# A recurrence's heads with other mixers' work between their steps: 2.0 units for each of their own instead of 1.15

## The chip, the cores and the metric

The kernel runs on one core of a Trainium2 chip. The metric is the device time of one launch in microseconds (us); the inputs lie in the chip's memory and the result is written there. The core has a matrix engine (TensorE, PE in the profile; PEld is its weight loading), a vector engine (VectorE, DVE), a scalar engine (ScalarE, ACT), a general one (GpSimd, POOL) and queues of DMA, most of which SyncE (SP) issues. Each engine works through its own list of instructions in order and waits at semaphores for the others.

## The reference

A sequence of 512 tokens of width 1024 goes through two layers of a first block (gated feed-forward, three mixers side by side, gated feed-forward) and two layers of a second block (three other mixers, then an MLP). Only the mixers of the first block matter here:

```python
def mixers(h):                              # one layer, S = 512, d = 1024
    z_a, z_b, z_c = split_cols(h @ w_in, [...])
    o_a = rwkv7_mixer(z_a, ...)             # 4 heads of 64, a recurrence in both directions
    o_b = mla_mixer(z_b, ...)               # latent attention, 8 heads
    o_c = retention_mixer(z_c, ...)         # 4 heads, in chunks
    return concatenate([o_a, o_b, o_c], -1) @ w_out

# rwkv7_mixer
    def step(state, inp):
        w_t, kk_t, kka_t, k_t, v_t, r_t = inp
        sk = einsum('dbhvk,dbhk->dbhv', state, kk_t)
        new = (state * w_t[..., None, :] - sk[..., :, None] * kka_t[..., None, :]
               + v_t[..., :, None] * k_t[..., None, :])
        ...
    y = head_norm(y, RWKV_LN_EPS) * ln_g + ln_b
    return (y + bonus).reshape(B, S, RWKV_WIDTH) * g
```

The recurrence (`rwkv7_mixer`) is computed for two directions and four heads, then normed by head, scaled, shifted, given a bonus term and gated. All of it is in f32.

## The kernel before

Activations lie transposed, 128 channels by 512 tokens. A large product is made of three fp32r matmuls: each operand is split into a rounded half (ACT) and its remainder (DVE, `split`, L446; `mix_r...` tiles in the profile). Weights come by DMA into `raw` and are split into pairs of `wr` tiles in the same way (`weight`, L385), some three ahead of their use. Small products are plain f32 matmuls, which the trace records twice. Nearly every instruction is issued through one helper (L138), so the trace's rows are told apart by tile names.

`mixer1` (L1441) computes the three mixers of a layer with Python generators that issue instructions and yield a number, the work that they have issued. `merge` (L1427) takes a main generator and a filling one. For every number that the main one yields it runs the filling one until that has yielded as much; what is left of the filling when the main one ends is issued at the end, and what is left of the main one when the filling ends follows without filling.

The main one is `rwkv` (L1111). After preparations it makes two generators `rwkv_heads` (L1042), one for each pair of heads (j = 0 and 1), and advances them by turns. Each does eight steps of the chunked recurrence; before every second step stands an `rwkv_pair` (L952), which prepares two steps. After the eighth come a square (ACT), a sum and an inverse root (`rsqrt`, L455, eleven small operations of DVE), a product, a broadcast (`head_bcast`, L744: one copy on DVE, four PE transposes), the bonus product, a gate matmul; then four transposes of y, a scaling from PSUM, an addition and the gate product (L1104 to L1108). Each generator yields 40 in all, 80 for both, and `rwkv` multiplies what they yield by `HEADS_FILL` (L1135).

The filling one (`fill`, L1453) issues the projections of the three mixers, then `retention` (L1377), then `mla` (L1249, latent attention). `mla` goes through eight heads, each with a first part (maxima of the scores, `mla_first`, L1177) and a second (`mla_second`, L1204: four blocks of three score matmuls, an exponential on ACT and four value matmuls of 65 columns), and transposes each pair of heads (`mla_pair`, L1235). At its last head it splits what the other two mixers have put out by then (`split_all`, L1304).

After `merge`, whatever isn't yet split is split (L1468), and `out_proj` (L418) multiplies by the output weights, eight blocks of 128 rows. The operands of each block are taken in the order `oa + oc + ob` (L1474): the recurrence's two outputs first, then the retention's two, then latent attention's four.

A scheduler orders each engine's instructions once more, within what the program's order and the buffers allow, so that independent matmuls of a later block can stand ahead of ones that have to wait.

Of the kernel before, what the change touches and what calls it, by code (L numbers as in the profile page):

```python
# [29 lines left out]
D_FF2 = 4096  # L30
NF2 = D_FF2 // P
FF_GROUPS = ((0, 8), (8, 7), (15, 7))
HEADS_FILL = 1.15
INV_WAIT = 20
HEAD_STEP = 1.5
INV_STEP = 2.5
# [199 lines left out]
class Build:  # L236
# [874 lines left out]
    def rwkv(self, l, z, dv, out):  # L1111
# [17 lines left out]
        while runs:  # L1129
            for g in list(runs):  # L1130
# [3 lines left out]
                else:  # L1134
                    yield need * HEADS_FILL  # L1135

# [864 lines left out]
```

## Time and profile before

| | us |
|---|---|
| median of three runs | 3496.72 (3494.79 to 3498.40) |
| profiled execution | 3498.36 |
| its span in the trace | 3496.6 |
| PE busy in it | 3398.2 |
| DVE busy | 2086.3 |
| ACT busy | 1427.3 |

The span is what the trace's clock covers from the first to the last instruction; all times in the rows count from its start. Busy time is the sum of an engine's instructions without overlap. Matmuls are pipelined and their ends are modelled, so a PE that is busy throughout can still hold pauses of some tenths of a us; they show in the distance from one start to the next. The granted clock of PE has two levels, 1.0 (2.4 GHz) and 0.5 (1.2 GHz); a stretch's figure is a mean of them. The mixers of the first block stand at about 410 to 810 us (layer 0) and 1560 to 1960 us (layer 1), their last third as described above at 583 to 800 and 1725 to 1945.

### The profile page before, as it was taken

To read this page: it belongs to the slowest core of one execution; us is meant where nothing else is said; L and a number is where in the kernel's file an instruction comes from. 1 tells how busy PE (TensorE), PEld (TensorE's weight loads), DVE (VectorE), ACT (ScalarE), POOL (GpSimd) and SP (SyncE) were. 2 spreads that over 40 slices of the span, in tenths; PEclk is the share of its full clock that TensorE was granted. 3 is DMA by queue.
4 is the path that set the end of the run, shared out by engine and by line. 5 is a ranking of instruction groups with operands and counts; after the bars stand their busy time and mean duration, and the time that the engine had idled before them with its cause. 6 is when DMAs were issued, how large, how long until landed. Compare 5 with 4: busy or idle time off the path is not lost. (4 is left out here: it accounts for less than half of the span.)

```text
span 3496.6 us, 45680 instructions
## 1 busy us (share of the span) xinstructions
PE 3398.2 (97%) x17394; PEld 2785.5 (80%) x17394; DVE 2086.3 (60%) x4249; ACT 1427.3 (41%) x2626; POOL 158.0 (5%) x272
## 2 busy tenths in 40 slices
PE   6999999999999999999999999999999999999998
PEld 5888877788888888887678888887788887778887
DVE  7954694767964544468476544467754446774445
ACT  3233554454233423245355423345443344443333
POOL 2000101001000000010100000000000000100000
PEclk9999998999999999999799999999999999999999
DMA  7933332016842222233201222221122222112222
GB/s 272 334 139 105 125 91 58 25 55 225 318 174 98 89 97 92 100 121 95 64 20 47 87 97 94 98 95 62 61 91 97 97 97 74 68 67 100 98 97 73
DMA packets 132876, 375.73 MB, mean 107 GB/s; under 512 B 37712, under 2 KB 41072, under 8 KB 132656
## 3 DMA queue, kind: packets, MB, share of 16 engines
q1 hardware_dynamic: 127808, 359.48, 29.8%
q0 software_dynamic: 3776, 12.32, 1.0%
q8 instruction: 136, 2.23, 0.3%
q10 hardware_dynamic: 1072, 1.01, 0.1%
q14 instruction: 84, 0.69, 0.1%
HBM read 362.27 MB, written 10.49 MB: 107 GB/s over the span
## 5 line engine op out<-in xcount | busy, mean ns | idle before, releaser
L138 ACT CAST wr<-raw 128x512 fp32r<-128x512 f32 (+2 forms) x1054 | 642.6, 611 | 1527.3 <-PE ps L138 1400.6
L138 DVE TENSOR_TENSOR wr<-raw,wr 128x512 fp32r<-128x512 f32 (+2 forms) x1048 | 707.5, 678 | 737.2 <-ACT wr L138 708.4
L138 PE MATMUL ps<-ff_h,wr 128*128 128x512 f32 (+1 forms) x4296 | 959.1, 385 | 12.5 <-ACT ff_h L138 8.2
L138 PEld LDWEIGHTS ps<-ff_h,wr 128*128 128x128 f32 x4296 | 792.8, 190 | 175.2 <-ACT ff_h L138 11.0
L138 PE MATMUL ps<-mlp_r,wr 128*128 128x512 f32 (+1 forms) x3120 | 699.4, 386 | 2.1 <-ACT mlp_r L138 2.1
L138 PEld LDWEIGHTS ps<-mlp_r,wr 128*128 128x128 f32 x3120 | 578.6, 188 | 121.2 <-ACT mlp_r L138 3.0
L138 PE MATMUL ps<-ff_r,wr 128*128 128x512 f32 (+1 forms) x2238 | 483.0, 377 | 0.0
L138 PEld LDWEIGHTS ps<-ff_r,wr 128*128 128x128 f32 x2238 | 403.6, 188 | 77.6
L138 PE MATMUL ps<-mix_r,wr 128*128 128x512 f32 (+1 forms) x1104 | 275.4, 400 | 3.3 <-DVE mix_s L138 1.7
L138 PE MATMUL ps<-mix_h_x,wr 128*128 128x512 f32 (+2 forms) x1104 | 260.6, 395 | 5.0 <-ACT mix_h_x L138 2.2
L138 PEld LDWEIGHTS ps<-mix_r,wr 128*128 128x128 f32 (+1 forms) x1104 | 200.6, 186 | 55.3 <-issue 3.5
L138 PEld LDWEIGHTS ps<-mix_h_x,wr 128*128 128x128 f32 (+1 forms) x1104 | 198.6, 196 | 52.8 <-issue 7.8
L138 DVE SCALAR_TENSOR_TENSOR ff_big<-ff_big,ff_big 128x1024 f32<-128x1024 f32 x144 | 175.9, 1234 | 12.6 <-DMA ff_big<-in_w_ada 12.4
L138 DVE SCALAR_TENSOR_TENSOR ff_s<-ff_s,ps 128x512 f32<-128x512 f32 x176 | 119.9, 682 | 82.7 <-PE ps L138 78.6
L138 DVE SCALAR_TENSOR_TENSOR x<-ps,hg,x 128x512 f32<-128x512 f32 (+1 forms) x102 | 73.2, 718 | 78.6 <-PE ps L138 78.5
L138 DVE TENSOR_TENSOR ps<-ps,mlp_s 128x512 f32<-128x512 f32 (+1 forms) x66 | 45.1, 683 | 100.3 <-PE ps L138 100.3
L138 DVE TENSOR_TENSOR mlp_r<-mlp_s,mlp_r 128x512 fp32r<-128x512 f32 x80 | 54.6, 691 | 68.2 <-ACT mlp_r L138 68.2
L138 PE MATMUL ps<-mix_s,mix_s 128*128 128x128 f32 (+6 forms) x632 | 87.5, 291 | 3.2 <-ACT mix_s L138 3.1
L138 ACT ACTIVATE mix_s<-ps,m 128x128 f32<-128x128 f32 (+3 forms) x130 | 65.4, 517 | 52.1 <-PE ps L138 28.1
L138 DVE TENSOR_REDUCE m<-ps 128x1 f32<-128x512 f32 (+4 forms) x132 | 74.8, 585 | 18.7 <-PE ps L138 18.2
L138 ACT COPY mix_s<-ps 64x128 f32<-64x128 f32 (+7 forms) x138 | 54.5, 399 | 74.8 <-PE ps L138 50.2
L138 PEld LDWEIGHTS ps<-mix_s,mix_s 128*128 128x128 f32 (+5 forms) x632 | 64.7, 175 | 21.5 <-ACT mix_s L138 12.6
(313 smaller groups left out, 3234.6 us busy)
## 6 DMA issues: line engine op xcount, KB each, us to landing
raw<-in_ff_in SPq DMA_DIRECT2D x176, 512.0 KB, 3.4
ff_big<-in_w_ada SPq DMA_DIRECT2D x144, 512.0 KB, 6.2
raw<-in_mlp SPq DMA_DIRECT2D x128, 512.0 KB, 3.4
raw<-in_ff_out SPq DMA_DIRECT2D x64, 448.0 KB, 3.2
raw<-in_ff_out SPq DMA_DIRECT2D x32, 512.0 KB, 3.8
raw<-in_out SPq DMA_DIRECT2D x32, 512.0 KB, 3.4
raw<-in_in SPq DMA_DIRECT2D x28, 512.0 KB, 3.4
raw<-in_in_a SPq DMA_DIRECT2D x18, 512.0 KB, 4.0
```

The lines of the kernel that those rows point to most:

```text
L138: self.alloc.last[self.name] = f(*a, **k)
```

## The change

```diff
-HEADS_FILL = 1.15
+HEADS_FILL = 2.0
```

Nothing else differs. Over the heads `rwkv` now yields 160 units for 80 of its own instead of 92. It concerns both layers of the first block, in the same way; the rest of the program stays as it is, but for buffer numbers. The order of the instructions follows from it, and these are three places of layer 0. In the names, `ps` are PSUM tiles, `mix_1_s` f32 tiles of the mixers, `mix_1_r`, `_r_x` and `_r_y` halves of split operands, `mix_1_va` the attention's values, `m` small columns; the last two numbers of a row are the shape that is written.

PE at the end of latent attention, before. The value matmuls of the last head, blocks 2 and 3, with the start of the projection around them; the four transposes by `ident` are the last `mla_pair`:

```order
L138 MATMUL ps_114<-mix_1_va_w_2_4744,mix_1_s_2669 128x65 x4
L138 MATMUL ps_113<-mix_1_r_x_3_4763,wr_74 128x512
L138 MATMUL ps_114<-mix_1_va_w_3_4745,mix_1_s_2677 128x65 x4
L138 MATMUL ps_113<-mix_1_r_x_2_4762,wr_74 128x512
L138 MATMUL ps_113<-mix_1_r_x_3_4763,wr_73 128x512
L138 MATMUL ps_113<-mix_1_r_y_1_4752,wr_74 128x512
L138 MATMUL ps_113<-mix_1_r_y_0_4751,wr_74 128x512
L138 MATMUL ps_117<-ident,mix_1_s_w_1_4747 128x128 x4
L138 MATMUL ps_113<-mix_1_r_y_1_4752,wr_73 128x512
L138 MATMUL ps_113<-mix_1_r_y_3_4754,wr_74 128x512
```

PE at the same place now. The two matmuls into `ps_116` are the last step of the second pair of heads; `mix_1_s_2678` and `mix_1_s_2683` are the broadcasts of the bonus, `mix_1_s_2674` the gates, `mix_1_s_2667` the last `mla_pair`, and `mix_1_s_2682` and `mix_1_s_2685` are y of the two pairs; `mix_1_r_y_5` and `_4` are the halves of the recurrence's first output:

```order
L138 MATMUL ps_116<-mix_1_s_2676,mix_1_s_2681 128x128 x2
L138 MATMUL ps_118<-mix_1_va_w_3_4591,mix_1_s_2668 128x65 x4
L138 MATMUL ps_112<-ident,mix_1_s_2678 128x128 x4
L138 MATMUL ps_119<-mix_1_s_2673,mix_1_s_2674 128x512
L138 MATMUL ps_117<-ident,mix_1_s_2667 128x128 x4
L138 MATMUL ps_113<-ident,mix_1_s_2683 128x128 x4
L138 MATMUL ps_115<-mix_1_s_2673,mix_1_s_2674 128x512
L138 MATMUL ps_114<-ident,mix_1_s_2682 128x128 x4
L138 MATMUL ps_118<-mix_1_r_y_5_4602,wr_74 128x512
L138 MATMUL ps_118<-mix_1_r_y_4_4601,wr_74 128x512
L138 MATMUL ps_118<-mix_1_r_y_5_4602,wr_73 128x512
L138 MATMUL ps_116<-ident,mix_1_s_2685 128x128 x4
```

The transposes of y stood 125 to 140 rows ahead of the projection's first matmul; now they stand directly before it and behind its first three. Six matmuls later comes the first one that takes the recurrence's second output.

DVE, before, at the end of the recurrence: `mix_1_s_2685` is y of the second pair, `mix_1_s_w_0` and `mix_1_s_2674` the two outputs, the rest is latent attention's and one weight:

```order
L138 TENSOR_REDUCE m_87<-ps_114 128x1
L138 TENSOR_TENSOR mix_1_s_2685<-mix_1_s_2685,m_94 128x512
L138 TENSOR_SCALAR mix_1_s_w_0_4746<-ps_112,vec 128x512
L138 TENSOR_SCALAR mr_104<-m_87 128x4
L138 TENSOR_TENSOR mix_1_s_w_0_4746<-mix_1_s_w_0_4746,mix_1_s_2677 128x512
L138 TENSOR_TENSOR wr_71<-raw_65,wr_72 128x512
L138 TENSOR_TENSOR mix_1_s_w_0_4746<-mix_1_s_w_0_4746,mix_1_s_2670 128x512
L138 TENSOR_SCALAR mix_1_s_2674<-ps_119,vec 128x512
L138 TENSOR_TENSOR mix_1_r_x_11_4771<-ps_118,mix_1_r_x_10_4770 64x512
L138 TENSOR_TENSOR mix_1_s_2674<-mix_1_s_2674,mix_1_s_2666 128x512
L138 TENSOR_TENSOR mix_1_r_x_13_4773<-ps_117,mix_1_r_x_12_4772 64x512
L138 TENSOR_TENSOR mix_1_s_2674<-mix_1_s_2674,mix_1_s_2682 128x512
```

DVE now: the end of the second pair's inverse root, the splits of the two outputs (`mix_1_r_y_4`, `mix_1_r_x_7`) and the first weight of the projection:

```order
L138 SCALAR_TENSOR_TENSOR m_87<-m_87,m_86 128x8
L138 SCALAR_TENSOR_TENSOR m_94<-m_87,m_94 128x8
L138 TENSOR_TENSOR m_87<-m_94 128x8
L138 TENSOR_TENSOR mix_1_r_y_4_4601<-mix_1_s_2666,mix_1_r_y_5_4602 128x512
L138 SCALAR_TENSOR_TENSOR m_87<-m_87,m_86 128x8
L138 SCALAR_TENSOR_TENSOR m_94<-m_87,m_94 128x8
L138 TENSOR_TENSOR mix_1_s_2685<-mix_1_s_2685,m_94 128x512
L138 TENSOR_SCALAR mix_1_s_2669<-ps_116,vec 128x512
L138 TENSOR_TENSOR mix_1_s_2669<-mix_1_s_2669,mix_1_s_w_1_4593 128x512
L138 TENSOR_TENSOR mix_1_s_2669<-mix_1_s_2669,mix_1_s_w_0_4592 128x512
L138 TENSOR_TENSOR mix_1_r_x_7_4613<-mix_1_s_2669,mix_1_r_x_6_4612 128x512
L138 TENSOR_TENSOR wr_73<-raw_64,wr_74 128x512
```

Latent attention's operations, which stood between those of the recurrence, are gone from the place, and the splits, which came some twenty rows later, follow at once.

PE at the end of the retention, before. `ident` with `mix_1_s_x` are the broadcasts of the retention's norm, `x_131` with `mix_1_s_2670` and `mix_1_s_2687` belong to a pair of the recurrence, and `mix_1_r_y` with `wr` is latent attention's first product:

```order
L138 MATMUL ps_115<-mix_1_s_2680,mix_1_s_x_0_4169 64x64 x8
L138 MATMUL ps_118<-x_131,mix_1_s_2670 128x128
L138 MATMUL ps_112<-ident,mix_1_s_x_2_4171 128x128 x4
L138 MATMUL ps_119<-ident,mix_1_s_x_3_4172 128x128 x4
L138 MATMUL ps_118<-x_131,mix_1_s_2670 128x128 x3
L138 MATMUL ps_114<-mix_1_s_2687,mix_1_s_2684 128x128
L138 MATMUL ps_117<-mix_1_r_y_0_4751,wr_74 128x512
```

Now:

```order
L138 MATMUL ps_115<-mix_1_s_2680,mix_1_s_y_3_2723 64x64 x8
L138 MATMUL ps_118<-x_134,mix_1_s_2668 128x128 x4
L138 MATMUL ps_115<-x_130,mix_1_s_2675 128x128 x4
L138 MATMUL ps_113<-ident,mix_1_s_x_0_4169 128x128 x4
L138 MATMUL ps_114<-ident,mix_1_s_x_2_4171 128x128 x4
L138 MATMUL ps_117<-mix_1_r_y_0_4597,wr_74 128x512
```

The pair's matmuls that stood between the broadcasts and the first product now stand ahead of the broadcasts.

## Rows read from the trace of the kernel before

**Rows 1.** The page, busy time of each engine, share of the span, instructions.
```profile
PE 3398.2 (97%) x17394; PEld 2785.5 (80%) x17394; DVE 2086.3 (60%) x4249; ACT 1427.3 (41%) x2626; POOL 158.0 (5%) x272
```

**Rows 2.** The page, chain that ended last, shares of the span by engine.
```profile
PE 42%; DVE 2%; ACT 1%; issue 0%; POOL 0%; DVEq 0%; ACTq 0%; POOLq 0%
```

**Rows 3.** Stretches: length; busy PE, PEld, DVE, ACT, POOL; granted PE clock; DMA.
```profile
583.00:647.00 64.00, 61.32 (x535) 45.31 (x533) 49.81 (x139) 28.02 (x71) 6.76 (x24) 1.00 0.01 2
647.00:693.00 46.00, 45.27 (x356) 37.64 (x356) 37.76 (x91) 28.25 (x62) 3.61 (x7) 1.00 0.14 47
693.00:713.00 20.00, 20.00 (x143) 17.81 (x144) 15.89 (x57) 9.21 (x16) 0.55 (x1) 1.00 0.05 14
713.00:763.00 50.00, 49.26 (x315) 41.92 (x313) 31.30 (x59) 29.99 (x52) 3.83 (x7) 1.00 0.19 59
...
1725.00:1790.00 65.00, 62.63 (x502) 43.39 (x500) 44.91 (x120) 26.21 (x65) 7.23 (x24) 0.95 0.02 6
```

**Rows 4.** PE's waits from 583 to 647 us: total, times, longest.
```profile
PE ps L138 <- ACT mix_s_y L138: 1.1, 1, 1.1
```

**Rows 5.** PE in order of time: start, length, operation, count; in the retention.
```profile
630.66 1.07 PE L138 MATMUL ps<-mix_s_x,mix_s 128*64 128x512 f32 x2
631.66 0.66 PE L138 MATMUL ps<-mix_s_x,mix_s_x 64*64 64x128 f32 x8
```

**Rows 6.** PE in order of time, around the end of the recurrence's last step.
```profile
703.53 0.66 PE L138 MATMUL ps<-mix_s,mix_s 128*128 128x128 f32 x4
...
704.67 0.61 PE L138 MATMUL ps<-mix_va_w,mix_s 128*128 128x65 f32 x4
705.11 0.61 PE L138 MATMUL ps<-ident,mix_s 128*128 128x128 f32 x4
705.56 1.02 PE L138 MATMUL ps<-mix_s,x 128*128 128x512 f32 x2
706.02 1.96 PE L138 MATMUL ps<-mix_r_x,mix_r_x 97*128 97x512 f32 x6
```

**Rows 7.** DVE in order of time, norm and gate of the recurrence's heads.
```profile
704.24 0.59 DVE L138 TENSOR_TENSOR mix_s<-mix_s,ps 64x128 f32<-64x128 f32 x2
...
707.31 0.42 DVE L138 TENSOR_TENSOR mix_s_w<-ps,m 128x256 f32<-128x256 f32 x1
...
708.53 0.48 DVE L138 SCALAR_TENSOR_TENSOR m<-m,m 128x8 f32<-128x8 f32 x4
...
709.04 0.69 DVE L138 TENSOR_TENSOR mix_s<-mix_s,m 128x512 f32<-128x512 f32 x1
709.65 0.68 DVE L138 TENSOR_TENSOR mix_r_x<-ps,mix_r_x 128x512 fp32r<-128x512 f32 x1
...
714.77 0.80 DVE L138 TENSOR_SCALAR mix_s_w<-ps,vec 128x512 f32<-128x512 f32 x1
...
720.49 0.67 DVE L138 TENSOR_TENSOR mix_s<-mix_s,mix_s 128x512 f32<-128x512 f32 x1
...
736.35 0.69 DVE L138 TENSOR_TENSOR mix_r_x<-mix_s_w,mix_r_x 128x512 fp32r<-128x512 f32 x1 [2.52 <-PE ps L138]
```

**Rows 8.** ACT in order of time, rounding of the recurrence's output.
```profile
735.70 0.62 ACT L138 CAST mix_r_x<-mix_s_w 128x512 fp32r<-128x512 f32 x1 [1.45 <-PE ps L138]
```

**Rows 9.** DVE in order of time, the retention's norm.
```profile
641.80 0.39 DVE L138 SCALAR_TENSOR_TENSOR m<-m,m 128x16 f32<-128x16 f32 x2
```

**Rows 10.** PE in order of time, start of the output projection.
```profile
762.93 0.48 PE L138 MATMUL ps<-mix_r_x,wr 128*128 128x512 f32 x1
...
767.12 3.57 PE L138 MATMUL ps<-mix_r_x,wr 128*128 128x512 f32 x15
```

**Rows 11.** Stretches as in rows 3, where the granted clock falls.
```profile
397.00:400.50 3.50, 0.98 (x7) 0.64 (x6) 2.84 (x13) 1.16 (x3) 1.19 (x3) 1.00 0.96 369
400.50:407.50 7.00, 6.51 (x29) 6.21 (x30) 6.04 (x20) 5.59 (x12) 2.74 (x4) 0.52 0.26 97
...
544.00:575.00 31.00, 29.37 (x256) 22.94 (x257) 4.37 (x8) 10.02 (x24) 2.77 (x8) 0.50 0.24 47
```

## The prediction

> **What bounds the kernel now.** I read the page first: TensorE (PE) is busy in 97% of the span [rows 1], and the chain that ended last lies on PE and hardly anywhere else [rows 2]. So a change of order can give only what PE idles, and takes whatever it makes PE wait. Then the stretches of one mixer, layer 0 [rows 3]: 583 to 647 us is the retention mixed with two thirds of the recurrence's pairs; 647 to 693 and 693 to 713 latent attention with the rest of the recurrence; 713 to 763 latent attention by itself; from 763 the output projection. PE idles 2.7 + 0.7 + 0.0 + 0.7 = 4.1 us in the four; the last row of the group, the retention's stretch in layer 1, is like layer 0's. The largest wait in the first stretch is 1.1 us [rows 4]. VectorE (DVE) has 49.8 of 64 us to do there and 31.3 of 50 in the stretch without recurrence. That difference is all that a better mixture can live on.
>
> Some idling is hidden in modelled ends: the retention's one f32 matmul (two records) at 630.66 has its successor at 631.66, 1.00 us later [rows 5], while a gate matmul of as many columns is followed after 0.46 [rows 6]. If all 16 such matmuls of a layer (2 pairs of heads, 4 blocks, 2 heads) hid the same 0.54, that is 8.6 us more. So a layer has between 4 and 13 us to be gained.
>
> **What is moved.** No instruction is added or removed in number; the main generator asks for 160 units of other work over its heads instead of 92. The retention stretch keeps two pairs and four steps of each head pair, and latent attention starts after them. But the filling work now ends before the main work: as the order shows, the last steps of the recurrence come immediately before latent attention's last value matmuls, and behind these there is nothing but the output projection, whose first operands are the recurrence's own outputs. Queues of DMA are passed by nothing: the weights' loads stand in the same order on SP.
>
> **Before, the recurrence's tail cost nothing.** Its last state add is at 704.24, its last gate product at 720.49 and the split of its outputs at 735.70 and 736.35, while the first projection matmul runs at 762.93 [rows 7, 8, 10]. The 17 us of norm, transposes and gate lay beside latent attention, and some 26 us were to spare.
>
> **The tail now, from the end of the second head pair's last step (T).** DVE's queue, as the order prints it, holds from there to the split of the last output: twelve passes over 128x512 at 0.61 (709.04 to 709.65), 7.3; two scalings from PSUM at 0.80, 1.6; the state add 0.59; a 128x256 product 0.42; ten small operations at 0.12 that are interleaved (four took 0.48), 1.2; and seven of a single chain at 0.2 (two took 0.39 in the retention's norm, where nothing stands between them), 1.4 [rows 7, 9]. Sum 12.5. It waits for two things: PE's transposes of the second pair, 0.45 and handovers, 0.6; and ScalarE's rounding of its output ahead of the last split, 0.62 and a handover, 0.7 [rows 8]. So T + 13.8 for the last split; the projection's three matmuls that need only the rounded half cover the last 0.6, and PE is wanted again from T + 13.2.
>
> PE's own work up to there: four value matmuls, eight records, 0.88 (four in 0.44); five times four transposes at 0.45, 2.25; two gate matmuls at 0.46, 0.92 [rows 6]; nine projection matmuls at 0.24 (fifteen took 3.57) [rows 10], 2.2. Sum 6.2. PE idles 13.2 - 6.2 = 7.0 us per layer, in four pieces: about 4 before the first output is rounded, 0.7 for its low half, 0.6 for the second product, 1.6 before the second output is rounded. Bounds: 6, if handovers vanish and everything overlaps; 9, if the ten interleaved operations cost 0.2 too and ScalarE's queue is late once.
>
> **The clock.** At 397 to 400.5 PE is busy for 0.98 of 3.5 us, and in the next 7 us the granted clock is 0.52, so nearly all of them run at the lower of its two levels, 1.2 instead of 2.4 GHz [rows 11]. The new tail has about 2 us of work in the 7 from T + 3 on, so I expect one such stretch behind it in each layer. It overlaps partly with the later pauses; with 3 us of work in it, doubled work costs 1.5. Ends: 0, and 3.5 for a full stretch of 7 us.
>
> **The seam.** Latent attention's first gemm now stands directly behind the retention's norm transposes; before, four 128x128 matmuls of a pair stood between, eight records of about 0.11 (four records of one step took 0.66, the last one's modelled end included) [rows 6], 0.9 us. That cover is gone: 0.9, ends 0 and 1.5.
>
> **The gain in the middle.** The stretch without recurrence gets steps to mix in, but it idles only 0.7. The retention stretch, where the idling is, loses filling: its DVE work stays while the pairs beside it go, so its mixture becomes denser on DVE, not thinner. I take 1.5 us gained per layer, near the recorded idling and not the hidden; ends 4 gained (all that is recorded) and 3 lost.
>
> Sum per layer: 7.0 + 1.5 + 0.9 - 1.5 = 7.9; two layers, 15.8. The profiled run took 3498.4 (span 3496.6), which is 1.6 above the median, so 3514 for it and **3513** against the median. Low end: 6 + 0 + 0 - 4 = 2 per layer, 3501; high end: 9 + 3.5 + 1.5 + 3 = 17, 3531.
>
> A rule that speaks for the change: the Trainium skill, "Perfetto Trace Analysis", section "Optimization Strategy", says that a kernel whose most contended engine changes over time may gain from interleaving its regimes. The trace has such regimes, 49.8 of 64 us on DVE against 31.3 of 50 [rows 3], but the one that is heavy on DVE is not the one that gets new partners. By the rule alone the sum would be rival A's.
>
> **Rivals.**
> A. The mixture wins. If all of the 13 us vanish, the rest (7.0 + 1.5 + 0.9 = 9.4) is paid back and 3.6 us per layer are left: 3490; with the tail at its floor and no slow clock, 3485. For: DVE's unequal load. Against: the gain would have to come from the stretch that loses partners. It decides from a gain of 9.4 per layer, twice my upper end. Chance 0.05.
> B. A wash. The tail at its floor of 6, no slow clock, a gain of 3 to 4: 3500 to 3503. Chance 0.14.
> C. The slow clock stays. From 544 to 575 PE had half the clock over 31 us, although it was busy for 29.4 of them [rows 11]. If the projection ran so for as long, 15 us more per layer: about 3540. Against: there the matmuls were small; behind the tail come dense ones of 512 columns. The Trainium skill, "TensorE: Matmul & The Clock Gate", section "What's actually happening", says that the throttled state is the default and that activity releases it, which by itself would favour a short stretch; the trace agrees for dense work, 7 us with PE busy in 6.5 of them from 400.5 on [rows 11]. Chance 0.06.
> D. The change doesn't do what it says, in time: the tail is covered by something the order doesn't show, say matmuls that PE still has in its queue. 3497. Against: behind the last value matmul nothing independent is left. Chance 0.03.
>
> **How the numbers follow.** The forecast (tail uncovered, 2 to 17 us per layer and over 0.2% in all) has 0.72. About 0.2%, 7 us, is what a measurement of this kernel can tell from no change: that is 3490 to 3504. Faster: A, 0.05. Within: B and D, 0.17. Slower: forecast and C, 0.78. The range, 3500 to 3530, takes in the bounds of the terms and most of B; A, C and D are left out.
>
> **What would show it.** Right: in both layers, between the last value matmuls and the projection, PE waits of about 4 and 1.6 us for ScalarE's mix_r and of 0.6 each for DVE; DVE without a gap through that time; granted clock of 0.5 behind it; the whole mixer longer by 8 us. Wrong: a tail without pauses over 1 us (then D or B); PE idling under 1 us and no 1.00 us spacing in the retention (then A); a projection at half clock for over 10 us (then C). The prediction falls if the four pieces add up to under 4 us, or if the retention's stretch changes by more than 4.

## The result and the profile after

The changed kernel takes 3534.2 us (median of four, 3528.4 to 3537.9) against 3497.6 (3494.8 to 3502.7): a ratio of 1.0107, with an interval of 1.0093 to 1.0122. It is slower, as forecast, but by 37 us instead of 16, and outside the range (3500 to 3530). The profiled execution is the fastest of the four: 3528.4, its span 3526.6. In it, the time from the start of the retention's stretch to the first product of the next block (583.3 to 812.0 in layer 0 before, 584.6 to 830.2 now) is 245.6 us in layer 0 and 247.1 in layer 1, against 228.7 in both before. These 16.9 and 18.4 us are nearly the whole loss; the two profiled executions differ by only 30.0 in all, as the changed one is 5 us shorter elsewhere.

The end of a mixer in layer 0, PE in order of time (start, length, operation, count, idle time before and what ended it), the counterpart of [rows 6, 10]:

```profile
770.38 1.00 PE L138 MATMUL ps<-mix_va_w,mix_s 128*128 128x65 f32 x8
...
774.26 0.66 PE L138 MATMUL ps<-ident,mix_s 128*128 128x128 f32 x4
778.42 0.50 PE L138 MATMUL ps<-mix_r_y,wr 128*128 128x512 f32 x1 [3.51 <-ACT mix_r_y L138]
779.26 1.22 PE L138 MATMUL ps<-mix_r_y,wr 128*128 128x512 f32 x2 [0.33 <-DVE mix_r_y L138]
780.27 1.10 PE L138 MATMUL ps<-ident,mix_s 128*128 128x128 f32 x4
781.03 2.20 PE L138 MATMUL ps<-mix_r_y,wr 128*128 128x512 f32 x6
784.44 2.15 PE L138 MATMUL ps<-mix_r_x,wr 128*128 128x512 f32 x8 [1.21 <-ACT mix_r_x L138]
```

The recurrence's last step ends at 770.4, then come the last value matmuls, broadcasts and gates, and the projection starts at 778.42 after a pause of 3.51 for ScalarE's rounding of the first output. Its second operand follows at 784.44 after 1.21. Layer 1 shows the same two, 3.53 and 1.04. From the last step to 784.44 are 14.1 us, with 5.05 of recorded pauses; before, PE had no pause there. DVE works through most of the time, with two pauses at the end, 1.21 for PE and 0.74 for ScalarE:

```profile
778.52 0.68 DVE L138 TENSOR_TENSOR mix_r_y<-mix_s,mix_r_y 128x512 fp32r<-128x512 f32 x1
...
779.51 0.69 DVE L138 TENSOR_TENSOR mix_s<-mix_s,m 128x512 f32<-128x512 f32 x1
781.41 0.81 DVE L138 TENSOR_SCALAR mix_s<-ps,vec 128x512 f32<-128x512 f32 x1 [1.21 <-PE ps L138]
782.26 1.42 DVE L138 TENSOR_TENSOR mix_s<-mix_s,mix_s_w 128x512 f32<-128x512 f32 x2
784.42 0.69 DVE L138 TENSOR_TENSOR mix_r_x<-mix_s,mix_r_x 128x512 fp32r<-128x512 f32 x1 [0.74 <-ACT mix_r_x L138]
```

These are the first output's split, the second pair's product, scaling, additions and split, the sequence that the order showed.

That is only a part of the loss. The retention's stretch in pieces (columns as in rows 3), which answers to the first of [rows 3]:

```profile
589.00:600.00 11.00, 10.64 (x56) 5.18 (x56) 9.45 (x16) 3.13 (x8) 1.36 (x4) 1.00 0.00 0
600.00:604.80 4.80, 4.44 (x60) 3.86 (x58) 4.04 (x12) 3.02 (x7) 1.77 (x5) 1.00 0.01 3
604.80:615.00 10.20, 10.20 (x43) 9.52 (x44) 5.91 (x25) 2.89 (x6) 0.00 (x0) 0.50 0.00 0
615.00:618.40 3.40, 1.24 (x8) 0.62 (x6) 2.85 (x7) 0.95 (x1) 0.00 (x0) 1.00 0.00 0
618.40:622.00 3.60, 3.60 (x7) 1.27 (x7) 2.82 (x11) 0.52 (x2) 0.00 (x0) 0.53 0.00 0
622.00:641.00 19.00, 18.83 (x153) 13.95 (x152) 12.08 (x34) 7.16 (x20) 2.55 (x12) 1.00 0.00 1
```

The granted clock was 1.00 through the whole stretch before. Now it is 0.50 from 604.8 to 615 and 0.53 from 618.4 to 622, nearly all of that time at 1.2 GHz. In layer 1 the stretch is 1.5 us longer still. What PE did before the clock fell:

```profile
601.12 0.67 PE L138 MATMUL ps<-mix_s_y,mix_s_x 64*64 64x128 f32 x16
602.15 1.05 PE L138 MATMUL ps<-masks,mix_s_x 128*128 128x2 f32 x8 [0.36 <-ACT mix_s_x L138]
603.06 1.03 PE L138 MATMUL ps<-ones,sq 128*128 128x1 f32 x8
604.02 0.67 PE L138 MATMUL ps<-mix_s_x,mix_s_x 64*64 64x128 f32 x16
604.62 1.87 PE L138 MATMUL ps<-mix_s_y,mix_s_y 128*128 128x64 f32 x8
...
617.73 0.74 PE L138 MATMUL ps<-mix_r,mix_r_x 128*128 128x512 f32 x2 [2.16 <-DVE x L138]
```

Small matmuls on 64 rows, then such of two columns and of one (the retention's head sums and the norms of latent attention's inputs), with a recorded pause of 0.36. From 604.62 on eight records of 64 columns take 1.87, where they take 1.00 at the full clock. The second fall stands behind a pause of 2.16 for DVE. In the kernel before, matmuls of 128 columns of a pair stand between the same narrow ones:

```profile
607.41 0.95 PE L138 MATMUL ps<-masks,x 128*128 128x2 f32 x8
608.29 1.16 PE L138 MATMUL ps<-mix_rw,mix_rw 64*128 64x128 f32 x16
...
609.54 0.95 PE L138 MATMUL ps<-ones,sq 128*128 128x1 f32 x8
```

Latent attention, 641 to 764, PE's waits (total, times, longest):

```profile
PE ps L138 <- DVE mix_r_y L138: 1.1, 1, 1.1
PE ps L138 <- ACT mix_s L138: 0.8, 1, 0.8
PE ps L138 <- ACT mix_r_x L138: 0.8, 1, 0.8
PE ps L138 <- ACT mix_r L138: 0.6, 1, 0.6
```

These four come to 3.3 us (two more have 0.3 and 0.2); the corresponding waits before, 0.7 up to 713 and 0.6 behind it. The first is the seam of the prediction.

### The profile page after: what moved, and what is told of

It reads as the page before. It is cut to its first block, busy times and chain, and to the rows that moved or that the text cites. A ratio compares the mean times of both kernels' runs of the same rounds, so it can differ in the third digit from the quotient of the medians.

```text
span 3526.6 us, 45685 instructions
## 1 busy us (share of the span) xinstructions
PE 3409.3 (97%) x17394; PEld 2793.1 (79%) x17394; DVE 2092.0 (59%) x4249; ACT 1428.3 (41%) x2626; POOL 155.4 (4%) x272
## 4 chain that ended last, share of the span: by engine, by line
PE 47%; DVE 5%; ACT 2%; issue 1%; DMA 1%; POOL 0%; DVEq 0%; ACTq 0%; SPq 0%
PE ps L138 47%; DVE mix_s L138 2%; DVE m L138 1%; ACT mix_s L138 1%; DVE wr L138 1%; ACT mix_r L138 1%; DVE x L138 0%; DVE mix_r L138 0%; DVE mix_big_w L138 0%; ACT wr L138 0%; DMA rw_d<-mix_big_w 0%; ACT mix_r_x L138 0%; DVE mlp_s L138 0%; DMA mix_big_w<-rw_d 0%; ACT L138 0%
## 5 line engine op out<-in xcount | busy, mean ns | idle before, releaser
L138 DVE SCALAR_TENSOR_TENSOR ff_big<-ff_big,ff_big 128x1024 f32<-128x1024 f32 x144 | 176.1, 1235 | 13.7 <-DMA ff_big<-in_w_ada 13.3
L138 PE MATMUL ps<-mix_s,mix_s 128*128 128x64 f32 (+7 forms) x704 | 95.9, 289 | 3.8 <-ACT mix_s L138 3.2
L138 PEld LDWEIGHTS ps<-mix_s,mix_s 128*128 128x128 f32 (+4 forms) x704 | 70.4, 171 | 22.5 <-ACT mix_s L138 12.1
L138 ACT COPY mix_s<-ps 128x256 f32<-128x256 f32 (+7 forms) x140 | 53.7, 393 | 70.0 <-PE ps L138 34.6
```

What stands on the lines that cost most here:

```text
L138: self.alloc.last[self.name] = f(*a, **k)
```

## Experiments

Each was timed beside the kernel before on the same chip, 3495.9 to 3497.6 us. The first two give `HEADS_FILL` two values, one while the filling is in the retention and one from latent attention on:

```diff
-                    yield need * HEADS_FILL
+                    yield need * HEADS_FILL[self.in_mla]
```

**The tail alone** (`HEADS_FILL = 1.15, 2.9`).

> 1.15 while the filling is still in the retention, 2.9 from latent attention on: the retention stretch is as before, the end of the recurrence runs out of filling as in the changed kernel. If the loss is the sum of an uncovered tail (7 us per layer) and a thinned retention (10 us per layer), this has the tail alone: about 3513 us, pauses of 3 to 4 and 1 to 2 us in front of the projection, and the granted clock of 1.0 from the first retention matmul on. If the tail with what it sets off behind it is the whole of the loss, it is 3534.

Measured: 3531.6 us, ratio 1.0098 (1.0079 to 1.0118). The retention was as before, with a clock of 1.00, and the pause ahead of the projection was there (3.7). But the start of latent attention, which now got its steps too sparsely, lost its clock:

```profile
588.00:646.00 58.00, 56.37 (x469) 41.20 (x468) 44.35 (x129) 22.92 (x61) 5.65 (x21) 1.00 0.00 1
646.00:666.40 20.40, 17.43 (x109) 13.44 (x108) 18.35 (x39) 16.29 (x36) 4.97 (x8) 1.00 0.08 26
666.40:683.40 17.00, 16.87 (x61) 14.44 (x61) 8.30 (x21) 2.36 (x4) 0.00 (x0) 0.50 0.18 63
```

17 us at half clock, with 61 records where the kernel before has 129 in the same 17 us. So this is not the tail alone, and 3513, which was expected for it, was missed. The run shows that too sparse a mixture costs in latent attention too; the size of the tail can't be read from it.

**The thinned retention alone** (`HEADS_FILL = 2.0, 0.8`).

> 2.0 in the retention, 0.8 from latent attention on: the retention is as thin as in the changed kernel, the tail is covered as before. If the thinned retention costs 10 us per layer by a clock that falls and by pauses, about 3517 us, with stretches of granted clock 0.5 between 585 and 625 us and no pause over 1 us in front of the projection. If the tail is the whole of the loss, 3497.

Measured: 3522.3, ratio 1.0077 (1.0061 to 1.0093). No recorded pause over 0.3 ahead of the projection, and the low clock in the retention:

```profile
592.40:596.00 3.60, 3.60 (x11) 2.40 (x12) 2.89 (x5) 0.11 (x1) 0.00 (x0) 0.53 0.00 0
616.30:623.20 6.90, 6.08 (x14) 3.00 (x15) 5.08 (x17) 0.52 (x2) 0.00 (x0) 0.51 0.00 0
```

A covered tail doesn't bring the time back. That the tail is not the whole loss follows only in part, since 0.8 makes a mixture of its own in latent attention, with a clock of 0.99 and 0.97 there in the two layers; the next runs show it without this.

**The projection with the recurrence's outputs last**, from the changed kernel and from the kernel before. In both the row table of the second block's projection was permuted too, so its values change, not its work.

```diff
-OUT1_ROWS = np.r_[0:256, 768:1024, 256:768]
+OUT1_ROWS = np.r_[768:1024, 256:768, 0:256]
...
-            self.out_proj(lambda j: self.wget(), oa + oc + ob, update, "halves")
+            self.out_proj(lambda j: self.wget(), oc + ob + oa, update, "halves")
```

> The changed kernel with the projection's operands in another order: the recurrence's two outputs last instead of first (the weight rows likewise). Eighteen of a block's 24 matmuls, 4 us for each of three blocks in flight, can then run under the tail. Uncovered tail and thinned retention: the tail's 7 us per layer go, the rest stays, about 3519 us. Tail alone: 3497 to 3500. If the pauses come back in front of the last six matmuls of each block, only a part of it.

> The kernel before with the same other order of the projection's operands: nothing waits there before, so nothing changes by either theory, 3497 us within 3 us. Should the order itself cost or give something, it is to be taken off the run with the changed kernel.

Measured: 3517.9 from the changed kernel (ratio to the kernel before 1.0064, 1.0045 to 1.0083), 3499.2 from the kernel before (1.0007, 0.9997 to 1.0016). The order itself does nothing clear of the noise; with it the changed kernel gets 16 us back by the medians, whose intervals leave some 8 us either way. The trace says it more closely: from the last value matmuls to the next block's first product are 48.0 us in the kernel before with either order, 59.1 in the changed kernel and 52.3 with the recurrence's outputs last, in both layers, so 6.8 per layer. PE at the same place:

```profile
774.90 0.66 PE L138 MATMUL ps<-ident,mix_s 128*128 128x128 f32 x4
775.31 0.94 PE L138 MATMUL ps<-mix_r_x,wr 128*128 128x512 f32 x3
...
781.60 0.66 PE L138 MATMUL ps<-ident,mix_s 128*128 128x128 f32 x4
```

The projection follows the transposes at once, and the second pair's transposes come 6.3 us later without a wait: eighteen matmuls of each block hide the tail. So the tail costs 6.8 us per layer with the slow clock that it sets off (5.05 of pauses, and up to 1.7 for the 3.4 us at half clock), where the prediction had 7.0 and 1.5. Some 22 us in all come from elsewhere.

**Dummy matmuls in the retention**, in the changed kernel and in the kernel before. `self.warm(pn)`, after the head sums of either pair and at every yield of the inputs' norms, multiplies the identity by itself six times into unused columns; the trace has 36 such matmuls in a layer, not the 30 expected:

```diff
+    def warm(self, pn):
+        for _ in range(6):
+            self.nc.tensor.matmul(pn[:, 128:256], self.ident, self.ident, start=True, stop=True)
```

> The changed kernel with five groups of six dummy matmuls (128 columns of the identity, into unused columns of a PSUM tile of the retention) among the retention's matmuls of 1 and 2 columns, where the granted clock falls at 604.8. They add some 3.3 us per layer at the full clock. If the clock falls because PE does next to nothing there, the stretches at 0.5 between 600 and 625 us go, and with them 5 us per layer: 3528 to 3531 us in all. If the low clock only follows pauses that wait for DVE, it stays, and the time is 3540.

> The kernel before with the same dummy matmuls. Its clock is at 1.0 there, so they can only cost: 3500 to 3504 us by either theory. Their price is to be taken off the run with the changed kernel.

Measured: 3528.0 in the changed kernel (1.0085, 1.0070 to 1.0100), 3503.8 in the kernel before (1.0018, 1.0008 to 1.0027). By the medians the dummies cost 6 us where the clock is up anyway and give 6 net where it falls, 12 us for the clock, with intervals that leave some 8 us either way. By the traces, from the retention's start to the next block, they cost 3.5 us per layer in the kernel before (232.2 against 228.7); the changed kernel with them has 244.6 in both layers, 1.0 and 2.5 less than without. So 4.5 and 6.0 us were the clock's, if the dummies cost the same in both kernels. The stretch with them:

```profile
600.00:605.00 5.00, 4.64 (x53) 4.27 (x51) 3.47 (x9) 2.92 (x5) 1.63 (x4) 1.00 0.01 3
605.00:615.00 10.00, 10.00 (x98) 9.62 (x98) 8.18 (x33) 3.05 (x5) 0.00 (x0) 1.00 0.00 0
615.00:640.00 25.00, 24.76 (x187) 17.41 (x186) 15.98 (x46) 8.60 (x25) 2.77 (x12) 1.00 0.01 1
```

```profile
602.71 1.58 PE L138 MATMUL ps<-ident 128*128 128x128 f32 x12
604.13 0.95 PE L138 MATMUL ps<-ones,sq 128*128 128x1 f32 x8
604.94 1.58 PE L138 MATMUL ps<-ident 128*128 128x128 f32 x12
...
608.49 1.00 PE L138 MATMUL ps<-mix_s_y,mix_s_y 128*128 128x64 f32 x8
```

The clock stays at 1.00, in layer 1 too, and the same eight records of 64 columns take 1.00 instead of 1.87. Nothing in the data flow was changed, and DVE had as much to do. The pauses ahead of the place are still there (0.9, 0.8 and 0.4 us); the one of 2.16 us behind it is gone. So it was PE's small work there that let the clock fall, not the waiting.

**Other factors**, 1.5, 1.0 and 1.3.

> A factor of 1.5: 120 units are asked of the 143 that the filling still has, so some 23 are left behind the last step and the tail is covered; the retention keeps 31 own units of the recurrence instead of 41 (before) and 24 (changed). If thinning costs by itself, about 3505 to 3512 us, with a granted clock of 0.5 for some us in the retention. If only the uncovered tail costs, 3497.

> A factor of 1.0: the retention gets more of the recurrence, latent attention is alone for longer. If thinning is what costs and the retention of the kernel before is already filled, this is within 4 us of 3497; if the trend goes on below 1.15, it is faster by 5 us or more. The tail-only theory expects 3497.

> A factor of 1.3: 36 own units in the retention instead of 41, nothing uncovered at the end. If each unit that is taken from the retention costs alike, a third of what 1.5 costs, about 3503 us. If the cost comes from single matmuls that lose their cover, and from where the clock happens to fall, it can be anything between 3497 and 3530, and the stretch of low clock in the profile says where.

Measured: 3515.7 (1.0049, 1.0034 to 1.0065), 3539.4 (1.0120, 1.0105 to 1.0135) and 3533.0 (1.0107, 1.0092 to 1.0122). All three missed what was expected of a smooth price per unit: 1.0 thickens the retention and costs the most, and 1.3 costs twice as much as 1.5. Each has its own place where the clock falls, in layer 0:

```profile
605.20:625.80 20.60, 20.60 (x81) 16.36 (x81) 10.76 (x41) 5.79 (x13) 0.00 (x0) 0.50 0.00 1
```

```profile
692.00:709.00 17.00, 17.00 (x62) 14.19 (x62) 5.79 (x17) 1.79 (x3) 0.00 (x0) 0.50 0.09 31
```

```profile
671.90:692.50 20.60, 20.60 (x79) 18.27 (x79) 8.62 (x24) 2.36 (x4) 0.00 (x0) 0.50 0.07 25
```

In the first it is the retention, in the other two the first third of latent attention. 1.15 is the one of the five values tried at which both mixtures hold the clock. The place is not fixed by the order alone: with 1.5 the retention's stretch, up to latent attention's first product, takes 71.3 us at a mean clock of 0.78 in layer 0 but 62.6 at 0.92 in layer 1, with the same matmuls in the same order.

**Only what the change is meant to do** (`HEADS_FILL = 1.15, 1.8`): retention as before, tail covered, the recurrence spread over more of latent attention.

> 1.15 in the retention, 1.8 from latent attention on: what the change says it does, and only that. The retention is as before, the recurrence's end is spread over more of latent attention, some 25 units are left to cover the tail. If the loss is made of the thinned retention and the uncovered tail, nothing of it is left: 3495 to 3500 us. If thinning costs in latent attention too, where PE then waits for maxima and rounding at its start, 3505 to 3520, with stretches of granted clock 0.5 between 660 and 710 us.

Measured: 3513.8, ratio 1.0049 (1.0032 to 1.0066). The intended part alone costs 18 us. PE there, and the same place in the kernel before:

```profile
665.94 1.15 PE L138 MATMUL ps<-mix_r_x,mix_r_x 96*128 96x512 f32 x4
669.22 1.10 PE L138 MATMUL ps<-x,mix_s 128*128 128x64 f32 x8 [2.13 <-DVE m L138]
...
671.82 1.84 PE L138 MATMUL ps<-mix_s,mix_s 128*128 128x64 f32 x8 [0.20 <-DVE mix_r L138]
```

```profile
667.78 1.15 PE L138 MATMUL ps<-mix_r_x,mix_r_x 96*128 96x512 f32 x4
668.87 1.60 PE L138 MATMUL ps<-mix_rw,mix_rw 64*128 64x128 f32 x16
```

```profile
664.00:672.00 8.00, 5.51 (x43) 4.50 (x41) 7.79 (x20) 2.04 (x5) 0.00 (x0) 1.00 0.30 116
672.00:686.00 14.00, 14.00 (x48) 12.22 (x49) 5.14 (x14) 2.02 (x4) 0.00 (x0) 0.51 0.11 37
```

Before, a pair's matmuls stood behind the first head's maxima. Now PE waits there 2.13 us for DVE (`m`, the maxima); the matmul that waits reads `x` and `mix_s` and not `m`, so by this row it waits for the PSUM buffer that a maximum is read from, not for the result. From 672 to 686 the clock is 0.51 with PE busy throughout: up to 7 of these 14 us are lost, in both layers at the same place. Latent attention takes 125.9 and 125.7 us from its first product to its last value matmuls, against 117.0 before, while the stretches on either side are as before; the pause and half of the slow time make up these 9 us per layer, though no run with the clock restored there shows it. The same pause stands ahead of the low clock with 1.3 and in the tail's run (1.8 and 1.5 us); with 1.0 none there is over 0.5.

**Both remedies in the changed kernel**, the other order of operands and the dummies.

> The changed kernel with both remedies, the projection's operands with the recurrence's last and the dummy matmuls in the retention. If tail (16 us by the run with the order alone) and low clock in the retention (6 us net of what the dummies add) are separate, both come off the changed kernel's 3534: 3511 to 3514 us. What is then left against 3497 is pauses at the start of latent attention and the dummies. If one of the two was already a part of the other, 3517 or more.

Measured: 3515.9, ratio 1.0058 (1.0043 to 1.0073), 2 us above the upper end expected. It lies between the two expectations, which its interval can't tell apart. Less the 6 that the dummies cost, 3510: 14 us above the kernel before of these runs (3495.9) are not of these two causes. Nor are they the clock's: from the retention's start to the next block it is 1.00 throughout, and that takes 237.8 us in both layers, 6.8 less than with the dummies alone and, less their 3.5, 5.6 more than before.

**Dummies in the pause before the first pairs**, in the kernel before: 32 in the first small step of `rwkv_blocks`, two in each later one.

```diff
+            self.warm(py, 32 if first and d == 0 else 2)
...
+            self.warm(pz, 2)
```

> The kernel before with 32 dummy matmuls in the pause of 4.2 us at 541 us, where PE waits for a transfer, and two in each small step behind it. There the clock falls to 0.5 for 17 to 41 us per layer and costs 3 to 6 us of it. If PE's doing nothing is what lets the clock fall, it stays at 1.0 up to 580 us, and the time is 3488 to 3495 us. If the narrow matmuls behind it (32 and 64 columns) are enough for it to fall, it falls a little later and the time is 3497 to 3503.

Measured: 3492.9, ratio 0.9990 (0.9980 to 0.9999), 3 us less than the kernel before and the fastest of all. The stretch, which answers to the last of [rows 11]:

```profile
541.00:546.00 5.00, 1.66 (x26) 1.47 (x25) 2.30 (x2) 3.29 (x4) 0.00 (x0) 1.00 1.01 210
546.00:575.00 29.00, 29.00 (x349) 24.43 (x347) 3.49 (x7) 9.24 (x22) 3.62 (x10) 0.88 0.18 39
```

The 32 dummies wait for nothing and ran ahead of the pause, 3.3 us of which remain. There they took the place of 29 of the projections' 512-column matmuls, which now run behind the pause, between the recurrence's small ones:

```profile
551.39 6.04 PE L138 MATMUL ps<-mix_h_x,wr 128*128 128x512 f32 x19
```

So three things changed at once, the work ahead of the pause, the wide matmuls and the pairs of dummies behind it, and the run doesn't show which of them held the clock. From 544 to 578 it was 0.50 before; now it is 0.90, some 27 us of half clock less. That only 3 us in all came of it is no sign that the clock matters little: the 46 dummies of a layer take 11 us of PE's time themselves. In layer 0 the pause is 0.9 shorter and the retention begins 2.4 us earlier, so the other work took some 13 us less, about half of the 27.

## Why the prediction was right in sign and wrong in size

**The tail** was right in mechanism and somewhat too large: 7.0 us of idling per layer in four pieces, T + 13.2 until PE is wanted again. The trace has 14.1 from the last step to the second output's matmul, and pauses of 3.5, 0.3 and 1.2, 5.0 in all, since part of the time went into projection matmuls at half clock. DVE had gaps where none was forecast. The run with the other operand order puts the tail's price at 6.8 us with the slow clock, against 8.5 forecast. The seam was right as well: 0.9 forecast, a wait of 1.1 for DVE. That the sign came out right is no luck, but tail and seam alone make up less than half of the loss.

**The gain in the middle** was the step that failed. I took 1.5 us gained per layer, with 3 lost as the bad end. By the traces a layer loses 16.9 and 18.4 us (245.6 and 247.1 against 228.7); without the tail's 6.8 and the seam's 1.1 the middle lost 9.0 and 10.5. I had seen that the retention's mixture would become "denser on DVE" and had looked for the price in PE's waits. Those grew only from 2.6 to 4.3 us in the retention's stretch.

**The clock** is what was missing in that step. I charged it to the tail alone, where I saw pauses coming, and left the middle at 1.00 because [rows 3] had it there. The dummies show 4.5 and 6.0 us for the retention's low clock in the two layers, more than the 3 that was my bad end; half of the slow time there (13.7 and 17.1 us) would be 6.8 and 8.5. That is also past the change of 4 in this stretch at which the prediction said that it falls. The clock fell behind matmuls of one and two columns that had lost the wider ones between them, with a list of waits that shows no pause over 0.4 us in the 15 us before. The rows that could have warned me were among those I read: from 544 to 575 the clock was at 0.50 with PE busy for 29.4 of 31 us [rows 11]. I used them for rival C, a slow projection, and not for the retention.

What is left is 3 to 6 us per layer, the seam included: 5.6 by the run with both remedies, 3.3 and 3.1 if the low clock cost half of its time. The waits in latent attention (3.8 us per layer in all rows against 1.3 before, the seam among them) hold 2.5 of it. For the rest the cause stays open; no run isolates it.

**The rivals.** A, the mixture wins, had it the wrong way round: with retention and tail kept, the spreading costs 18 us. The rule of the Trainium skill behind it ("Perfetto Trace Analysis", section "Optimization Strategy", regimes that are interleaved may gain) names a possible gain, and none came of it here: the regimes were interleaved already, and four other shares than 1.15 cost 18 to 42 us. B and D are out, since 3534 lies clear of 3497. C named the right mechanism and the wrong place: the projection recovered its clock after short stretches (0.72 from 778.4 to 784.4, 0.94 from there to 840). The Trainium skill, "TensorE: Matmul & The Clock Gate", section "What's actually happening", has the throttled state as the default that activity releases. The trace agrees, and the dummy matmuls in the retention do so most plainly: 0.50 without them, 1.00 with them.

## What to carry to other kernels

When work that fills another chain's gaps is moved elsewhere, look at the place that it leaves: which narrow matmuls lose their wide neighbours there, and what the granted clock does in stretches of the same trace that already look like that. The price of a filling factor need not be a slope (1.0, 1.15, 1.3, 1.5 and 2.0 gave 3539, 3498, 3533, 3516 and 3534 us), so one value on each side should be measured before a trend is believed. Where medians leave several us open, compare the same stretch in both traces: from the retention's start to the next block it took the same time within 0.1 us in both layers of the kernel before. And an operand that is ready last belongs last in an accumulation, where its lateness has the other operands to hide behind.

## What the hardware showed that was not expected

The granted clock fell to 0.5 although PE had no recorded pause over 0.4 us from 589.3 on, behind 3.5 us of matmuls on 64 rows and of two and one columns (601.1 to 604.6), and stayed there for 10 us. In a layer, 36 dummy matmuls of 128 columns kept it at 1.00 and paid for themselves: by the traces they cost 7 us in the two layers and gave 10.5. In the kernel before, dummies around a pause for a transfer, with wide matmuls moved behind it, raised the clock there from 0.50 to 0.88.
